# Triangular inverses of a two-layer decoder: 16x16 diagonal blocks made row by row on VectorE, then three doubling steps instead of six

## The chip, the cores and the metric

The kernel runs on one core of one Trainium2 chip. A core has TensorE (PE: matmuls and transposes, with a separate weight load, PEld), VectorE (DVE), ScalarE (ACT), GpSimd (POOL), SyncE (SP, which issues the DMAs here) and 16 DMA engines. Each engine works through its own instructions in order and waits on semaphores for the others. The metric is the device time of one execution in microseconds; the median of several runs counts.

## The reference

The kernel computes two decoder layers on x of 256 tokens by 2048 features in fp32. Layer 0 mixes tokens with mLSTM heads and RWKV-7 heads, layer 1 with retention heads and gated DeltaNet heads; each mixer is followed by a SwiGLU block.

```python
for layer in range(DEPTH):
    h = x * (1.0 + scale) + shift
    y = _mixer_ab(h, ...) if layer % 2 == 0 else _mixer_cd(h, positions, ...)
    x = _layer_norm(ALPHA * x + (1.0 + gate) * y, ln_g[layer, 0], ln_b[layer, 0])
    y = _swiglu(x * (1.0 + scale) + shift, ffn_w_gate[layer], ffn_w_up[layer], ffn_w_down[layer])
    x = _layer_norm(ALPHA * x + (1.0 + gate) * y, ln_g[layer, 1], ln_b[layer, 1])
```

Two of the mixers are delta rules: the state is corrected at each token by what it already holds. RWKV-7 has it as a recurrence, DeltaNet in chunks with a triangular solve:

```python
S = S * wt[:, :, None, :] + sa[..., None] * bt[:, :, None, :] + vt[..., None] * kt[:, :, None, :]   # sa = S at
...
ut = jnp.eye(CHUNK, dtype=f32) + jnp.where(strict, jnp.einsum('cbhtd,cbhsd->cbhts', kb, kc) * gamma, 0.0)
u = lax.linalg.triangular_solve(ut, vc * bc[..., None], left_side=True, lower=True)
```

The kernel writes both in chunks of 128 tokens, and so needs, for each head and chunk, the inverse of a 128x128 unit triangular matrix. There are 16 RWKV heads and 8 DeltaNet heads, two chunks each.

## The kernel before

**Products.** Every large product goes through `product` and `unit` (L342 to L368). A unit takes 512 rows of a weight matrix, 1 MB, by DMA into one of three `raw` buffers. `split` (L327) makes two halves of it: ScalarE rounds a half to fp32r (`hi`, L337) and VectorE makes the rest (`lo = raw - hi`, L338); there are three buffers of each. Per half TensorE runs four groups of three matmuls (L357 to L359: activations' high part by `hi` and by `lo`, low part by `hi`) into two PSUM banks of the kind `g`, of which there are four. Between units, `fill` puts in the modulation's products: 1 MB of `ada` weights goes through the same `raw` buffers, and one VectorE instruction multiplies and sums it (L289).

**Order.** The program is traced in order, and a scheduler sorts the instructions into each engine's queue ahead of the run by priority, which is the place in the program; `high_priority(offset=n)` moves a block n instructions ahead. The splits have an offset of 2000. What comes later in the program, such as a following product, is put beside earlier work where its buffers allow it. On the chip each queue is then run strictly in that order.

**The heads.** `rwkv` (L864) takes the 16 RWKV heads in four batches of four heads. `rwkv_batch` and `rwkv_front` prepare a batch (L708, L724 to L761), with the transposes of the columns in `rwkv_tiles` (L691). `rwkv_heads` (L763) computes the scores (L776), copies them with ScalarE into `mk[:, 0]` and `mk[:, 1]` (L777, L778), masks them with GpSimd (`keep_upper` L642, `unit_diagonal` L646), calls `inverses` on `mk[:, 0]` (8 matrices: four heads by two chunks) and goes on with the state and the output (L794 to L848). `gdn_group` (L1051) does the same for two groups of four DeltaNet heads, with the scores written by VectorE into `ma[:, 0]` (L1109) and the inverse used at L1136; `ma[:, 1]` is used at L1141.

**The inverse.** `inverses` (L600) keeps the inverse `d` and its transpose `dt`, each 128 x 8 x 128, and doubles the size of the inverted diagonal blocks. Start: eight transposes of `mt` (L611), of which VectorE keeps the 2x2 blocks (L612, mask `m2`), while GpSimd keeps those of `mt` itself in `dt` (L613, mask `m2t`). Then follow six levels, for block sizes 2, 4, 8, 16, 32 and 64. A level multiplies `mt` by the blocks (L622), masks (L626, `lev`), multiplies by `dt` (L629), adds into `d` (L632), transposes `d` (L636) and copies it into `dt` with ScalarE (L637). Each level works on two halves of four matrices. A 128x64 fp32 matmul is two instructions in the trace, so a level has 16 of L622, 16 of L629 and 8 of L636.

Of the kernel before, what the change touches and what calls it, by code (L numbers as in the profile page):

```python
# [13 lines left out]
AF = mybir.ActivationFunctionType  # L14
ALU = mybir.AluOpType
# [4 lines left out]
P = 128  # L20
# [9 lines left out]
LN_EPS = 1e-5  # L30
DH = 128
DECAY = -math.exp(-0.5)
LEVELS = (2, 4, 8, 16, 32, 64)


COLS = {}
# [7 lines left out]

CONS = {}
_n = 0
for _name, _w in [("ident", 128), ("cum", 256), ("tr", 128), ("ones", 128), ("sl", 128), ("m2", 128), ("m2t", 128),
                  ("lev", 64 * len(LEVELS)), ("bones", 128), ("hsel", 2), ("freq", 64)]:
    CONS[_name] = (_n, _w)
    _n += _w  # L50
# [3 lines left out]
def constants():  # L54
    i = np.arange(P)
    c = np.zeros((P, NCONS), np.float32)

    def put(name, a):
        o, w = CONS[name]
        c[:, o:o + w] = a  # L60

    u, t = i[:, None], i[None, :]
# [4 lines left out]
    put("tr", u <= t)  # L67
    put("ones", 1.0)
    put("sl", u > t)
    put("m2", (u // 2 == t // 2) & (t <= u))  # L70
    put("m2t", (u // 2 == t // 2) & (u <= t))
    lev = []
    for b in LEVELS:
        j = np.arange(64)
# [6 lines left out]
    s, t = i[:, None].astype(np.float64), np.arange(T)[None].astype(np.float64)  # L81
    ret = np.zeros((8, P, 384), np.float32)
    for h in range(8):
        lg = np.log1p(-np.exp2(-5.0 - h))
        e = np.where(t >= s, np.exp(lg * np.maximum(t - s, 0.0)), 0.0) * DH ** -0.5
# [100 lines left out]
class Trunk:  # L186
# [413 lines left out]
    def inverses(self, mt, dd):  # L600


        nc, v = self.nc, self.nc.vector
        d, dt = dd[:, 0], dd[:, 1]
        halves = [slice(0, 4), slice(4, 8)]
        m2, m2t = (self.con(n).unsqueeze(1).to_broadcast([P, 4, P]) for n in ("m2", "m2t"))
        four = lambda x: x.rearrange("p (h t) -> p h t", h=4)
        for hs in halves:
            b = self.bank()
            for j in range(4):  # L610
                nc.tensor.transpose(b[:, P * j:P * j + P], mt[:, hs.start + j, :], self.ident)  # L611
            v.tensor_tensor(d[:, hs, :], four(b[:]), m2, ALU.mult)  # L612
            nc.gpsimd.tensor_tensor(dt[:, hs, :], mt[:, hs, :], m2t, ALU.mult)  # L613
        lev = self.con("lev")
        for n, size in enumerate(LEVELS):
            dv = d.rearrange("p h (n two b) -> p h n two b", two=2, b=size)
# [23 lines left out]
    def keep_upper(self, x, dims, strict):  # L640

        self.nc.gpsimd.affine_select(x, x, pattern=[[0, n] for n in dims] + [[1, P]], compare_op=ALU.is_gt if strict else ALU.is_ge,  # L642
                                     fill=0.0, base=0, channel_multiplier=-1)

    def unit_diagonal(self, x, n):
        self.nc.gpsimd.affine_select(x, x, pattern=[[0, n], [1, P]], compare_op=ALU.not_equal, fill=1.0, base=0, channel_multiplier=-1)  # L646


    def shifted(self, out, src, mu, rows=P):
# [113 lines left out]
    def rwkv_heads(self, B):  # L763
# [6 lines left out]
        for t in range(NT):  # L770
            for c, h in heads:
                r = slice(64 * h, 64 * h + 64)
                j = 4 * t + 2 * c + h
                b = self.bank()
                for x in range(2):
                    mm(b[:, T * x:T * x + T], bk[r, c, x, t, :], ar[r, c, t].rearrange("p x s -> p (x s)"), start=True, stop=True)  # L776
                nc.scalar.activation(mk[:, 0, j, :], b[:, 0:P], AF.Copy, scale=rho[:, t, 2 * c + h:2 * c + h + 1])  # L777
                nc.scalar.activation(mk[:, 1, j, :], b[:, 2 * P:3 * P], AF.Copy)  # L778
                v.tensor_copy(rbkr[:, j], b[:].rearrange("p (k x s) -> p k x s", k=2, x=2)[:, :, 1, :])
            js = slice(4 * t, 4 * t + 4)  # L780
            self.keep_upper(mk[:, :, js, :], [2, 4], True)
            self.unit_diagonal(mk[:, 0, js, :], 4)
            self.keep_upper(rbkr[:, js], [4, 2], False)
        dt = self.inverses(mk[:, 0], self.y8([P, 2, 8, P]))
        V = B["vb"][:, 0]
# [265 lines left out]
    def gdn_group(self, g, product, rest, gates=None):  # L1051
# [43 lines left out]
        for t in range(NT):  # L1095
# [13 lines left out]
                    v.scalar_tensor_tensor(ma[:, 0, 4 * t + i + j, :], bv[:, j, 0, :], wn[:, t, i + j:i + j + 1], gam[:, i + j, :], ALU.mult, ALU.mult)  # L1109
                v.tensor_tensor(ma[:, 1, 4 * t + i:4 * t + i + 2, :], bv[:, :, 1, :], gam[:, i:i + 2, :], ALU.mult)  # L1110
            js = slice(4 * t, 4 * t + 4)
            self.keep_upper(ma[:, 0, js, :], [4], True)
            self.unit_diagonal(ma[:, 0, js, :], 4)
            self.keep_upper(ma[:, 1, js, :], [4], False)
        dt = self.inverses(ma[:, 0], self.a8([P, 2, 8, P]))
        rest()
# [233 lines left out]
```

## Time and profile before

| | |
|---|---|
| median of the runs | 2915.05 us |
| lowest and highest of 3 runs | 2909.9, 2915.27 us |
| the profiled execution | 2917.53 us |
| its span, first to last instruction | 2914.8 us |
| mean granted clock of TensorE | 0.976 |
| calls of `inverses` | 4 (RWKV), 2 (DeltaNet) |
| the calls, first L611 to last L636 start | 230 to 279, 319 to 364, 407 to 451, 501 to 546, 1691 to 1738, 1823 to 1875 us |

The profile is of one execution on the chip. In a row of groups stand the line, the engine, the operation, output<-input with their shapes, the count, then the busy time in us and the mean of one in ns, and behind a second bar the idle time of the engine just ahead of those instructions with what ended it. In a timeline a row begins with its start and its length in us; a bracket gives the idle time before it and its releaser. Weight loads lie beside matmuls, and a matmul's length holds the time that it takes through the array, so the issue time of a batch is read from the start of what follows. Durations below are of this execution.

### The profile page before, as it was taken

Reading aid. Unit: us, or ns where it says so; the run is one execution under the profiler, and the core shown is the slowest. Engines: PE = TensorE matmul, PEld = TensorE weight load, DVE = VectorE, ACT = ScalarE, POOL = GpSimd, SP = SyncE. Lnnn points to the kernel's source line nnn. Section 1 sums busy time; section 2 is a strip of 40 time slices with the busy share of each in tenths; the row PEclk is TensorE's granted clock in tenths of the full one; section 3 lists DMA queues with packets and bytes.
Section 4 is the critical chain, followed back from the end, with each engine's and each line's share of the span. In section 5 each row is a group of like instructions: output and inputs, shape, how many; then the busy total and the mean of one; then the engine's idle time right before and its main releaser. Section 6 shows DMA issues by size and latency. Waiting matters only on the chain.

```text
span 2914.8 us, 34843 instructions
## 1 busy us (share of the span) xinstructions
PE 2760.8 (95%) x13466; PEld 2291.6 (79%) x13466; DVE 2011.9 (69%) x2955; ACT 1276.3 (44%) x1685; POOL 123.5 (4%) x114
## 2 busy tenths in 40 slices
PE   3699999999999999999998999999989999999997
PEld 2578887877778888888887888877878888888886
DVE  7876666687777557767758878687786545556556
ACT  2264345446454444444445545343444444443442
POOL 0001111020000000000000121101000000000000
PEclk9799999999999999999999999999999999999998
DMA  9974234367578668867855756477656656667563
GB/s 366 356 277 170 91 134 159 131 242 267 199 249 305 249 219 296 297 236 275 305 197 205 295 209 241 159 277 295 216 202 231 249 195 224 242 220 241 192 216 130
DMA packets 106189, 674.62 MB, mean 231 GB/s; under 512 B 12068, under 2 KB 14248, under 8 KB 28328
## 3 DMA queue, kind: packets, MB, share of 16 engines
q1 hardware_dynamic: 106024, 672.41, 64.1%
q8 instruction: 105, 1.72, 0.2%
q14 instruction: 60, 0.49, 0.0%
HBM read 663.97 MB, written 8.39 MB: 231 GB/s over the span
## 4 chain that ended last, share of the span: by engine, by line
PE 62%; DVE 5%; DMA 3%; issue 1%; ACT 1%; POOL 1%; POOLq 0%; DVEq 0%; ACTq 0%
PE g L359 19%; PE g L358 19%; PE g L357 19%; DMA raw<-ada 2%; DVE lo L338 2%; DVE raw L289 1%; PE m L622 1%; PE m L629 1%; PE m L575 1%; ACT hi L337 1%; DMA raw<-gu 1%; DMA raw<-w_cd 0%; PE m L524 0%; PE c L317 0%; PE m L636 0%
## 5 line engine op out<-in xcount | busy, mean ns | idle before, releaser
L338 DVE TENSOR_TENSOR lo<-raw,hi 128x1024 fp32r<-128x1024 f32 (+2 forms) x848 | 1025.4, 1215 | 653.6 <-ACT hi L337 650.3
L337 ACT ACTIVATE hi<-raw 128x1024 fp32r<-128x1024 f32 (+2 forms) x848 | 885.7, 1049 | 1165.6 <-PE g L359 1004.1
L357 PE MATMUL g<-hi,h 128*128 128x512 f32 (+3 forms) x2368 | 932.7, 396 | 80.3 <-ACT hi L337 76.5
L358 PE MATMUL g<-lo,h 128*128 128x512 f32 (+3 forms) x2368 | 934.1, 395 | 3.8 <-DVE lo L338 3.8
L359 PE MATMUL g<-hi,h 128*128 128x512 f32 (+3 forms) x2368 | 930.9, 394 | 0.0
L357 PEld LDWEIGHTS g<-hi,h 128*128 128x128 f32 x2368 | 451.9, 191 | 172.0 <-ACT hi L337 78.8
L358 PEld LDWEIGHTS g<-lo,h 128*128 128x128 f32 x2368 | 452.6, 191 | 95.2 <-DVE lo L338 9.1
L359 PEld LDWEIGHTS g<-hi,h 128*128 128x128 f32 x2368 | 452.0, 191 | 88.6 <-issue 2.7
L289 DVE SCALAR_TENSOR_TENSOR raw<-raw,silu_c 128x2048 f32<-128x2048 f32 x176 | 404.4, 2298 | 23.1 <-DMA raw<-ada 22.8
L359 PE MATMUL g<-hi,a 128*128 128x512 f32 x960 | 374.5, 390 | 0.0
L357 PE MATMUL g<-hi,a 128*128 128x512 f32 x960 | 374.4, 390 | 0.0
L358 PE MATMUL g<-lo,a 128*128 128x512 f32 x960 | 374.1, 390 | 0.1
L358 PEld LDWEIGHTS g<-lo,a 128*128 128x128 f32 x960 | 180.3, 188 | 37.4 <-DVE lo L338 0.5
L359 PEld LDWEIGHTS g<-hi,a 128*128 128x128 f32 x960 | 180.3, 188 | 36.9
L357 PEld LDWEIGHTS g<-hi,a 128*128 128x128 f32 x960 | 180.2, 188 | 37.0
L1099 POOL TENSOR_SCALAR s<-cons_sb,log_alpha 128x128 f32<-128x128 f32 x16 | 22.9, 1446 | 1040.6 <-PE g L359 903.4
L637 ACT ACTIVATE y<-m 128x512 f32<-128x512 f32 x48 | 27.4, 595 | 78.3 <-PE m L636 78.1
L902 DVE SCALAR_TENSOR_TENSOR f<-c,cols_sb,f 128x255 f32<-128x255 f32 (+2 forms) x120 | 57.2, 477 | 6.2 <-ACT f L900 5.1
L626 DVE TENSOR_TENSOR P<-m,cons_sb 128x256 f32<-128x256 f32 x72 | 30.1, 423 | 43.6 <-PE m L622 43.2
L629 PEld LDWEIGHTS m<-P,y 128*128 128x128 f32 x384 | 50.0, 203 | 2.1 <-issue 0.3
L622 PEld LDWEIGHTS m<-y,a 128*128 128x128 f32 x384 | 49.7, 205 | 0.8
L622 PE MATMUL m<-y,a 128*128 128x64 f32 x384 | 49.7, 283 | 0.0
(376 smaller groups left out, 2051.2 us busy)
## 6 DMA issues: line engine op xcount, KB each, us to landing
raw<-ada SPq DMA_DIRECT2D x176, 1024.0 KB, 5.5
raw<-gu SPq DMA_DIRECT2D x176, 1024.0 KB, 4.8
raw<-dn SPq DMA_DIRECT2D x88, 1024.0 KB, 4.8
raw<-w_cd SPq DMA_DIRECT2D x60, 1024.0 KB, 5.0
raw<-w_ab SPq DMA_DIRECT2D x56, 1024.0 KB, 5.5
a<-ada SPq DMA_DIRECT2D x16, 1024.0 KB, 11.3
raw<-o_ab SPq DMA_DIRECT2D x16, 1024.0 KB, 5.0
raw<-o_cd SPq DMA_DIRECT2D x16, 1024.0 KB, 4.9
```

The lines of the kernel that those rows point to most:

```text
L289: v.scalar_tensor_tensor(w[:], w[:], 1.0, self.sc[:], ALU.mult, ALU.mult, accum_out=m[:, i:i + 1])
L337: nc.scalar.activation(hi[:, :2 * n], ws, AF.Copy)
L338: nc.vector.tensor_tensor(lo[:, :2 * n], ws, hi[:, :2 * n], ALU.subtract)
L357: mm(o, ah, wh, start=first, stop=False)
L358: mm(o, ah, wl, start=False, stop=False)
L359: mm(o, al, wh, start=False, stop=stop and k == 3)
L575: nc.tensor.transpose(b[:, P * k:P * k + P], gs[:, t, P * k:P * k + P], self.ident)
L622: nc.tensor.matmul(x[:, 64 * j:64 * j + 64], mt[:, hs.start + j, :], dv[:, hs.start + j, :, 0, :], start=True, stop=True)
L626: v.tensor_tensor(p[-1][:], four(x[:, 0:256]), mask, ALU.mult)
L629: nc.tensor.matmul(x[:, 256 + 64 * j:320 + 64 * j], dt[:, hs.start + j, :], y[:, j, :], start=True, stop=True)
L637: nc.scalar.activation(dt[:, hs, :], four(x[:]), AF.Copy)
L902: v.scalar_tensor_tensor(o[:, d:T], z[:, 0:T - d], self.col(wname, c + 3 - d), o[:, d:T], ALU.mult, ALU.add)
```

## The change

The inverses of the 16x16 diagonal blocks are made on VectorE, and the doubling starts at size 16. Per call:

- `e2` takes the two 16x16 diagonal blocks of each 32x32 diagonal block of `mt`, for 32 partitions at a time, times a strictly triangular mask (`tri`); their sum `u` holds, for each partition, the row of its own block, 128 x 8 x 16.
- `e` starts as `u` plus the unit diagonal (`diag`). For k from 14 down to 1 a shuffle brings row k of each block to all 16 partitions of the block, the copy is multiplied by column k of `u`, and the product is added into `e`, all for the columns beyond k. That block has a priority offset of 4000.
- `dt` is `e` spread over the block diagonal by the mask `blk`, and `d` its transpose by TensorE, copied by ScalarE.
- The levels of sizes 2, 4 and 8 go, and with them their part of `lev`, the masks `m2` and `m2t`, GpSimd's product at L613, and `unit_diagonal`. `keep_upper` stays for the second matrix alone (`mk[:, 1]`, `ma[:, 1]`); the first is now read without a mask.

```diff
-LEVELS = (2, 4, 8, 16, 32, 64)
+BASE = 16
+LEVELS = (16, 32, 64)
...
-    put("m2", (u // 2 == t // 2) & (t <= u))
-    put("m2t", (u // 2 == t // 2) & (u <= t))
+    c32, c16 = np.arange(32)[None], np.arange(BASE)[None]
+    put("tri", (u % 32 // BASE == c32 // BASE) & (u % BASE < c32 % BASE))
+    put("diag", u % BASE == c16)
+    put("blk", u // BASE == np.arange(P // BASE)[None])
...
     def inverses(self, mt, dd):
         nc, v = self.nc, self.nc.vector
         d, dt = dd[:, 0], dd[:, 1]
         halves = [slice(0, 4), slice(4, 8)]
-        m2, m2t = (self.con(n).unsqueeze(1).to_broadcast([P, 4, P]) for n in ("m2", "m2t"))
         four = lambda x: x.rearrange("p (h t) -> p h t", h=4)
+        with self.tc.high_priority(offset=4000):
+            e2 = self.t1([P, 8, 2, BASE])
+            for q in range(4):
+                r = slice(32 * q, 32 * q + 32)
+                o = CONS["tri"][0]
+                v.tensor_tensor(e2[r], mt[r, :, r].rearrange("p h (a c) -> p h a c", a=2),
+                                self.cons[r, o:o + 32].rearrange("p (a c) -> p a c", a=2).unsqueeze(1).to_broadcast([32, 8, 2, BASE]), ALU.mult)
+            u, e, f = (self.own([P, 8, BASE], "e1", 3) for _ in range(3))
+            v.tensor_tensor(u[:], e2[:, :, 0, :], e2[:, :, 1, :], ALU.add)
+            v.tensor_tensor(e[:], u[:], self.con("diag").unsqueeze(1).to_broadcast([P, 8, BASE]), ALU.add)
+            for k in range(BASE - 2, 0, -1):
+                n = BASE - 1 - k
+                x = f[:, :, k + 1:]
+                v.stream_shuffle(x, e[:, :, k + 1:], [k] * 16 + [16 + k] * 16)
+                v.tensor_tensor(x, x, u[:, :, k:k + 1].to_broadcast([P, 8, n]), ALU.mult)
+                v.tensor_tensor(e[:, :, k + 1:], e[:, :, k + 1:], x, ALU.add)
         for hs in halves:
+            v.tensor_tensor(dt[:, hs, :].rearrange("p h (n c) -> p h n c", c=BASE), e[:, hs, :].unsqueeze(2).to_broadcast([P, 4, 8, BASE]),
+                            self.con("blk").unsqueeze(1).unsqueeze(3).to_broadcast([P, 4, 8, BASE]), ALU.mult)
             b = self.bank()
             for j in range(4):
-                nc.tensor.transpose(b[:, P * j:P * j + P], mt[:, hs.start + j, :], self.ident)
-            v.tensor_tensor(d[:, hs, :], four(b[:]), m2, ALU.mult)
-            nc.gpsimd.tensor_tensor(dt[:, hs, :], mt[:, hs, :], m2t, ALU.mult)
+                nc.tensor.transpose(b[:, P * j:P * j + P], dt[:, hs.start + j, :], self.ident)
+            nc.scalar.activation(d[:, hs, :], four(b[:]), AF.Copy)
...
-            self.keep_upper(mk[:, :, js, :], [2, 4], True)
-            self.unit_diagonal(mk[:, 0, js, :], 4)
+            self.keep_upper(mk[:, 1, js, :], [4], True)
...
-            self.keep_upper(ma[:, 0, js, :], [4], True)
-            self.unit_diagonal(ma[:, 0, js, :], 4)
             self.keep_upper(ma[:, 1, js, :], [4], False)
```

More of the change, by code (lines that the diff above doesn't have):

```diff
@@ L46 @@
 _n = 0
-for _name, _w in [("ident", 128), ("cum", 256), ("tr", 128), ("ones", 128), ("sl", 128), ("m2", 128), ("m2t", 128),
+for _name, _w in [("ident", 128), ("cum", 256), ("tr", 128), ("ones", 128), ("sl", 128), ("tri", 32), ("diag", 16), ("blk", 8),
                   ("lev", 64 * len(LEVELS)), ("bones", 128), ("hsel", 2), ("freq", 64)]:
@@ L643, in keep_upper @@
                                      fill=0.0, base=0, channel_multiplier=-1)
-    def unit_diagonal(self, x, n):
-        self.nc.gpsimd.affine_select(x, x, pattern=[[0, n], [1, P]], compare_op=ALU.not_equal, fill=1.0, base=0, channel_multiplier=-1)
     def shifted(self, out, src, mu, rows=P):
```

## The prediction

> **What bounds the kernel now.** I read the page's busy shares first, then its chain, then the two stages that call `inverses`, then the waits of TensorE there.
>
> ```profile
> PE 2760.8 (95%) x13466; PEld 2291.6 (79%) x13466; DVE 2011.9 (69%) x2955; ACT 1276.3 (44%) x1685; POOL 123.5 (4%) x114
> ...
> PE 62%; DVE 5%; DMA 3%; issue 1%; ACT 1%; POOL 1%; POOLq 0%; DVEq 0%; ACTq 0%
> ...
> L338 DVE TENSOR_TENSOR lo<-raw,hi 128x1024 fp32r<-128x1024 f32 (+2 forms) x848 | 1025.4, 1215 | 653.6 <-ACT hi L337 650.3
> L337 ACT ACTIVATE hi<-raw 128x1024 fp32r<-128x1024 f32 (+2 forms) x848 | 885.7, 1049 | 1165.6 <-PE g L359 1004.1
> L289 DVE SCALAR_TENSOR_TENSOR raw<-raw,silu_c 128x2048 f32<-128x2048 f32 x176 | 404.4, 2298 | 23.1 <-DMA raw<-ada 22.8
> ```
>
> TensorE (PE) is busy 95% of the span and carries 62% of the chain that ended last; VectorE (DVE) carries 5%. ScalarE's `hi` copies wait 1004.1 us for TensorE to finish with a buffer (L359): the three split buffers are usually full, so weights wait for TensorE and not the other way round. What is taken from TensorE's queue is therefore worth its full length wherever other work can move up. The stages that matter, by windows of all engines:
>
> ```profile
> 230.00:560.00 330.00, 317.60 (x2052) 274.40 (x2053) 202.28 (x463) 145.79 (x279) 39.47 (x36) 0.96 0.36 127
> 1690.00:1880.00 190.00, 185.72 (x1126) 160.57 (x1124) 140.25 (x254) 80.19 (x129) 27.60 (x24) 0.97 0.54 195
> ```
>
> The columns are PE, weight loads, DVE, ACT, POOL, granted clock, DMA share. Four calls of `inverses` lie in the first window, two in the second. TensorE is busy 96% and 98%, VectorE 61% and 74%, the DMA engines 36% and 54%. So inside the stages too TensorE is the bound, and VectorE has some room, though not much in the second. The idle rest of TensorE has mostly one cause:
>
> ```profile
> L611 PE MATMUL m<-cons_sb,a 128*128 128x128 f32 x48 | 8.1, 297 | 16.9 <-POOL a L646 16.9
> L646 POOL TENSOR_SCALAR_AFFINE_SELECT a<-a 128x512 f32<-128x512 f32 x12 | 17.6, 1465 | 0.4
> ...
> 230.22 0.66 PE L611 MATMUL m<-cons_sb,a 128*128 128x128 f32 x4 [1.93 <-POOL a L646]
> 235.15 0.66 PE L611 MATMUL m<-cons_sb,a 128*128 128x128 f32 x4 [2.59 <-POOL a L646]
> ```
>
> The first transposes of each inverse (L611) wait for GpSimd's masks, 16.9 us in all six calls.
>
> **What the change takes from TensorE.** One level in the first call, in the timeline of TensorE; what stands behind each batch gives its issue time:
>
> ```profile
> 265.42 1.90 PE L622 MATMUL m<-y,a 128*128 128x64 f32 x16
> 267.13 0.47 PE L358 MATMUL g<-lo,h 128*128 128x512 f32 x1
> ...
> 268.14 1.89 PE L629 MATMUL m<-P,y 128*128 128x64 f32 x16
> 269.84 0.47 PE L359 MATMUL g<-hi,h 128*128 128x512 f32 x1
> ...
> 270.39 1.03 PE L636 MATMUL m<-cons_sb,y 128*128 128x128 f32 x8
> 271.26 1.90 PE L622 MATMUL m<-y,a 128*128 128x64 f32 x16
> ```
>
> The steps are 267.13 - 265.42 = 1.71 us, 269.84 - 268.14 = 1.70 us and 271.26 - 270.39 = 0.87 us: 4.28 us per level. Three levels fewer (2, 4 and 8) in six calls are 18 x 4.28 = **77.0 us**. The first eight transposes of a call stay; only their source changes from `mt` to `dt`.
>
> The masks on POOL leave the path: `mt` goes into the new chain, and into L622, unmasked (the level masks `lev` clear the rest), so the **16.9 us** of waits go. POOL's remaining mask of `mk[:, 1]` or `ma[:, 1]` serves L794 or L1141, after the inverse, and is costed at nothing: the levels hide it; without them its price would be that of such a mask, 1.5 us. The constants shrink by 392 columns, 128 x 392 x 4 bytes = 0.2 MB; by
>
> ```profile
> DMA packets 106189, 674.62 MB, mean 231 GB/s; under 512 B 12068, under 2 KB 14248, under 8 KB 28328
> ```
>
> that is 0.9 us at most, at the start; I count nothing.
>
> **What it adds on VectorE.** Prices, from dependent small operations on 128x8 (start to start) and from larger ones by size:
>
> ```profile
> 301.00 0.17 DVE L412 TENSOR_TENSOR v<-v 128x8 f32<-128x8 f32 x1
> 301.20 0.17 DVE L413 TENSOR_TENSOR v<-v,v 128x8 f32<-128x8 f32 x1
> 301.40 0.17 DVE L414 TENSOR_SCALAR v<-v 128x8 f32<-128x8 f32 x1
> ...
> L626 DVE TENSOR_TENSOR P<-m,cons_sb 128x256 f32<-128x256 f32 x72 | 30.1, 423 | 43.6 <-PE m L622 43.2
> ...
> L612 DVE TENSOR_TENSOR y<-m,cons_sb 128x512 f32<-128x512 f32 x8 | 5.5, 690 | 8.9 <-PE m L611 8.9
> L632 DVE TENSOR_TENSOR y<-m,y 128x256 f32<-128x256 f32 x48 | 20.3, 424 | 25.2 <-PE m L629 24.8
> ```
>
> The slope is (690 - 423) / 256 = 1.04 ns per element; a dependent operation on 128x8 takes 0.20 us from start to start, so its fixed part is 0.192 us. The chain has 14 rows, k from 14 to 1, each a shuffle, a product and a sum on 8 x n elements, n from 1 to 14: 42 x 0.192 + 3 x 840 x 0.00104 = 8.1 + 2.6 = 10.7 us. Ahead of it are four 256-element products (4 x 0.42 = 1.7 us, as L626) and two 128-element sums (0.33 us each): 13.1 us. No row shows a shuffle. I bound it by 0.17 us (L413's duration, already in the sum) and by twice that if a lane list is loaded first, 14 x 0.17 = 2.4 us more; I take the middle, so the chain is **14.3 us** (13.1 to 15.5) of VectorE time per call. The two `blk` products (0.69 us) replace the two of L612. Gone are six L626 and six L632, 12 x 0.42 = 5.1 us. Net +9.2 us per call, 55 us in all: VectorE would go from 2012 to about 2067 us. ScalarE loses six L637 copies and gains two of the same shape:
>
> ```profile
> L637 ACT ACTIVATE y<-m 128x512 f32<-128x512 f32 x48 | 27.4, 595 | 78.3 <-PE m L636 78.1
> ...
> 228.94 0.29 ACT L778 ACTIVATE a<-m 128x128 f32<-128x128 f32 x1
> ...
> 256.93 1.00 PE L622 MATMUL m<-y,a 128*128 128x64 f32 x8
> ```
>
> That is 2.4 us less per call, on an engine with room: nothing.
>
> The Trainium skill speaks against the trade: VectorE: DVE Perf Modes, section "Rules for kernel authors", says of chained DVE operations to keep their count low, since each pays its fixed part. The trace agrees, with 0.192 of 0.20 us fixed on 128x8. By that page's 2400 ns for a shuffle of 2048 elements, less 2048 x 1.04 ns, a shuffle's fixed part is an estimated 0.27 us; the sum would stay as it is.
>
> **What of it lies on the path.** In call one the last score copy (L778) ends at 229.2 us, and the size-16 level, which stays, starts at 256.9 us (L622): 27.7 us. After the change the same stretch holds about 1 us until VectorE is free (half of a 2.3 us L289), 14.3 us of chain, 0.7 us of `blk` product: 16 us to the first transpose, then 1 to 2 us of transposes and copies. So the latency shortens as well, but TensorE now needs 16 us of other work where it has no level to do. Queued behind the chain on VectorE (it has priority 4000, the splits 2000) are L338's `lo` halves and L289; whoever waits for `lo` is the product on TensorE. Its cover is the three full split buffers, 12 matmuls each:
>
> ```profile
> 248.65 0.39 PE L358 MATMUL g<-lo,h 128*128 128x512 f32 x1
> 248.88 0.40 PE L359 MATMUL g<-hi,h 128*128 128x512 f32 x1
> ...
> 237.39 0.63 PE L358 MATMUL g<-lo,h 128*128 128x512 f32 x1
> 237.82 0.63 PE L359 MATMUL g<-hi,h 128*128 128x512 f32 x1
> ```
>
> At 0.23 us from start to start that is 36 x 0.23 = 8.3 us, and some 2.7 us of the next batch's L708, L691 and L724, 11 us in all. So I put a wait of 16 - 11 = **5 us per call**, 30 us in six. Both ends: nothing, if splits slip in between the dependent rows of the chain and keep TensorE fed; 16 us, if TensorE finds nothing at all.
>
> **The sum.** -77.0 - 16.9 + 30 = -63.9 us. Its profiled execution took 2917.5 us (span 2914.8), which gives 2853.6; the median of the runs, 2915.05, lies 2.5 us lower, so I forecast **2851 us**.
>
> The slow clock after a wait is costed at nothing, since there are waits before and after. Its price: behind the waits at 230 and 235 us the products start 0.43 us apart instead of 0.23 (last fence), and the granted clock of 0.96 over the 330 us of four calls makes 330 x 0.04 / 4 = 3.3 us per call. The Trainium skill, in TensorE: Matmul & The Clock Gate, section "Part 1: The HAM clock gate", puts the slow half at idle windows of some 3.4 us; here two shorter gaps, 1.93 and 2.59 us with some work between, were followed by it, so the trace asks for less. By the page a 5 us wait would always pay it, by the trace also.
>
> **Rivals.**
> (a) The chain is wholly covered: splits are issued between its dependent rows, as other work stands between the steps of a root here:
>
> ```profile
> 297.67 0.17 DVE L409 TENSOR_SCALAR v<-v 128x8 int32<-128x8 int32 x1
> 297.74 0.42 DVE L748 TENSOR_TENSOR y<-f,f 128x256 f32<-128x256 f32 x1
> 298.08 0.16 DVE L410 TENSOR_SCALAR v<-v 128x8 int32<-128x8 int32 x1
> ...
> DVE  7876666687777557767758878687786545556556
> ```
>
> Then -77.0 - 16.9 = -93.9 us, and without the slow clock up to -93.9 - 6 x 3.3 = -114: 2801 to 2821 by the runs, say 2815. For it: L748 starts 0.07 us behind L409, so each dependent step leaves 0.13 us free. Against: it needs nearly all of VectorE's room.
>
> (b) VectorE becomes the bound of the two stages. Its work there would be 202.3 + 4 x 9.2 = 239 us and 140.3 + 2 x 9.2 = 159 us. The last row above is its busy share in fortieths of the span: 8 tenths at most. At 80% the stages take 299 and 199 us in place of 330 and 190: 31 - 9 = 22 us less, 2893. For it: 74% now in the second stage. Against: L289s can move to later products.
>
> (c) Slower: a transpose placed in TensorE's queue ahead of ready products stands there for the whole chain, and they behind it. Price: 16 us and 3.3 us of slow clock per call, 116 us; -93.9 + 116 = +22 us, 2937. It decides from 93.9 / 6 = 15.7 us of lost time per call. For it: L611 stood so for POOL. Against: POOL's waits average 16.9 / 6 = 2.8 us per call, and the buffers are full.
>
> (d) It doesn't do what it says: the freed 77 us is only waited out elsewhere, since the head work behind each inverse sets the pace; within 0.2%, 2915. Against: TensorE 96% busy.
>
> **How the numbers follow.** Forecast 0.52, (a) 0.22, (b) 0.15, (c) 0.07, (d) 0.04. Measurement of this kernel tells some 0.2% (6 us) from no change. Faster is the forecast, (a) and most of (b), 0.88; same is (d) and a little of (b), 0.05; slower is (c), 0.07. The range goes from 2810, within (a), to 2893, the price of (b); a third of (a), some of (b), and (c) and (d) stay outside, about 0.2.
>
> **What would show it.** Right: no L622, L629 or L636 for three levels (576, 576 and 288 instructions become half); no POOL releaser at the first transposes; VectorE near 2067 us; TensorE's busy time some 77 us less, weight loads and matmuls together; waits of a few us, on VectorE or the `dt` product, ahead of six groups of transposes; levels starting some 18 to 25 us after the last L778. Wrong: rows of the chain far above 0.2 to 0.3 us; long gaps of TensorE beside the chain with L338 late; the granted clock lower in both stages; VectorE past 85% there.

## The result, and the profile after

| | before | after |
|---|---|---|
| median of 4 runs, us | 2915.16 (2909.9 to 2918.53) | 2867.9 (2864.73 to 2871.11) |
| profiled execution, us (span) | 2917.53 (2914.8) | 2870.56 (2868.8) |
| mean granted clock | 0.976 | 0.969 |
| TensorE busy, us | 2760.8 | 2692.8 |
| VectorE busy, us | 2011.9 | 2041.5 |
| first layer norm, behind layer 0's mixer, starts at, us | 794.74 | 776.21 |
| layer 1's mixer, from the start of the second norm to that of the third, us | 603.4 | 574.2 |

The kernel is faster by 1.6%: the ratio is 0.984, with an interval of 0.9819 to 0.986. That is 47 us, where 64 were forecast; the time lies inside the range of 2810 to 2893. The last two rows of the table say where the 17 us are missing. The two calls of `inverses` in layer 1 brought 29 us, about 14.6 each. The four in layer 0 brought 18.5 us, 4.6 each.

The page of after, its busy shares, the granted clock in fortieths of the span, and the chain that ended last:

```profile
PE 2692.8 (94%) x12746; PEld 2215.4 (77%) x12746; DVE 2041.5 (71%) x3255; ACT 1263.7 (44%) x1664; POOL 82.5 (3%) x86
...
PEclk9799798899999999999999999999999999999998
...
PE 77%; DVE 14%; DMA 5%; issue 2%; ACT 2%; POOL 0%; POOLq 0%; SPq 0%; DVEq 0%; ACTq 0%
```

TensorE is still the bound, but VectorE carries 14% of the chain in place of 5%, and the granted clock falls to 7 and 8 tenths in the fifth, seventh and eighth slice (290 to 360 and 430 to 570 us), which lie in layer 0. The same row before has a 9 in all of them:

```profile
PEclk9799999999999999999999999999999999999998
```

The same two stages by windows of all engines (us, then PE, weight loads, DVE, ACT, POOL, granted clock, DMA share, GB/s), before:

```profile
170.00:794.70 624.70, 605.64 (x3374) 502.11 (x3374) 441.24 (x896) 302.33 (x505) 64.59 (x62) 0.98 0.51 184
1600.00:2150.00 550.00, 534.99 (x2806) 449.34 (x2804) 435.85 (x740) 249.99 (x353) 58.75 (x48) 0.98 0.66 240
```

and after, each window ending at the same event:

```profile
170.00:776.20 606.20, 562.96 (x2891) 453.04 (x2890) 464.45 (x1096) 295.34 (x490) 41.23 (x46) 0.94 0.52 189
1581.50:2103.70 522.20, 509.64 (x2566) 423.79 (x2566) 443.18 (x841) 245.27 (x346) 41.08 (x36) 0.98 0.69 253
```

In layer 1 TensorE's busy time fell by 25.4 us, the six levels of two calls (6 x 4.28 = 25.7), and its idle time (window less busy) from 15.0 to 12.6 us: the change worked there as if it were covered completely. In layer 0 the twelve levels should have taken 51.4 us off TensorE. Its busy time fell by only 42.7, so what stayed ran 8.7 us slower (granted clock 0.94 in place of 0.98), and its idle time grew from 19.1 to 43.2 us, though the waits for POOL are gone. -51.4 + 8.7 + 24.1 is the 18.6 us that the stage got shorter.

What TensorE waited for, in the view of waits of after (total us, times, longest):

```profile
PE m L853 <- ACT t L848: 8.6, 2, 8.0
PE g L361 <- DVE lo L341: 7.9, 15, 1.2
PE c L708 <- DVE e L624: 7.7, 2, 5.9
PE c L911 <- DVE v L418: 7.6, 1, 7.6
...
PE c L708 <- DVE e L625: 3.7, 1, 3.7
...
PE m L632 <- DVE y L628: 0.2, 1, 0.2
```

L632 are the first transposes of an inverse, where I expected waits of 5 us per call: they wait 0.2 us in all. The waits are at other places, in the work that follows the inverses of layer 0: at the tail (L853), at the token transposes of a later product (L708) and at the conv (L911). Here is why, in the timeline of VectorE in the middle of call one's rows (start, duration):

```profile
236.31 0.18 DVE L624 STREAM_SHUFFLE e<-e 128x16 f32<-128x16 f32 x1
236.39 2.27 DVE L292 SCALAR_TENSOR_TENSOR raw<-raw,silu_c 128x2048 f32<-128x2048 f32 x1
...
238.59 0.17 DVE L625 TENSOR_TENSOR e<-e,e 128x16 f32<-128x16 f32 x1
238.68 1.21 DVE L341 TENSOR_TENSOR lo<-raw,hi 128x1024 fp32r<-128x1024 f32 x1
239.82 0.17 DVE L626 TENSOR_TENSOR e<-e,e 128x16 f32<-128x16 f32 x1
...
243.53 0.19 DVE L625 TENSOR_TENSOR e<-e,e 128x32 f32<-128x32 f32 x1
243.75 0.19 DVE L626 TENSOR_TENSOR e<-e,e 128x32 f32<-128x32 f32 x1
```

Two dependent operations of a row can start 0.22 us apart (last two lines). But in the order in which VectorE's queue was laid out, a modulation row of 2.27 us or a `lo` half of 1.21 us stands between many of them. The chain of call one starts at 229.12 us and its `blk` product at 267.40 us. The windows of that stretch, for all engines, for L341 and for L292 alone:

```profile
229.00:268.40 39.40, 36.02 (x159) 28.07 (x159) 38.74 (x101) 16.88 (x21) 2.04 (x3) 1.00 0.79 294
...
229.00:268.40 39.40, 13.38 (x11) 1.00 0.79 294
...
229.00:268.40 39.40, 11.64 (x12) 1.00 0.79 294
```

VectorE is busy 38.74 of 39.40 us, 13.38 of them with splits and 11.64 with the modulation. TensorE meanwhile is fed (36.0 of 39.4 us, clock 1.00). From the chain's start to the first transposes call one takes 39.3 us, the other calls of layer 0 20.1, 28.8 and 29.1 us, those of layer 1 54.5 and 41.5 us. So no wait stands at the transposes, and in three of layer 0's four calls the inverse is late instead. From the last score copy to the tail's first matmul (L794 before, L810 after) the four calls took 50, 47, 44 and 46 us before, and 66, 43, 51 and 57 us after; the second, with the shortest chain, comes a little sooner. TensorE has nothing else to do when the tail, the token transposes and the next batch come late:

```profile
316.19 0.47 PE L853 MATMUL m<-cons_sb,t 128*128 128x128 f32 x1 [7.97 <-ACT t L848]
...
336.90 1.09 PE L708 MATMUL c<-cons_sb,zt 128*128 128x128 f32 x4 [3.69 <-DVE e L625]
...
434.53 1.09 PE L708 MATMUL c<-cons_sb,zt 128*128 128x128 f32 x4 [5.88 <-DVE e L624]
...
500.38 1.09 PE L911 MATMUL c<-cons_sb,zt 128*128 128x128 f32 x4 [7.63 <-DVE v L418]
```

The releaser that stands behind L708 is a row of the next inverse, but the transposes don't read it. They need a bank of PSUM (`c`) that the token shift (L670, with L669 on ScalarE) has read, and L670 stands among the rows on VectorE. The timeline of all engines shows it, with the wait of L669 in brackets:

```profile
432.80 0.47 DVE L670 SCALAR_TENSOR_TENSOR z<-c,cols_sb,z 128x255 f32<-128x255 f32 x1
...
433.30 0.47 ACT L669 ACTIVATE z<-c,one_less_mu 128x256 f32<-128x256 f32 x1 [3.56 <-DVE z L670]
...
433.91 0.48 DVE L670 SCALAR_TENSOR_TENSOR z<-c,cols_sb,z 128x255 f32<-128x255 f32 x1
434.31 0.01 DVE L624 LOAD_MASK_SELECT e<-e  x1
```

The last L670 ends at 434.39 us, and L708 starts at 434.53. Around such gaps the clock is low: a window of all engines over the first of them shows TensorE busy for 25.59 us of 40, at 0.66.

```profile
300.00:340.00 40.00, 25.59 (x108) 18.52 (x108) 21.58 (x85) 13.56 (x41) 3.93 (x5) 0.66 0.17 60
```

### The profile page after: what moved, and what is told of

Read it like the earlier page. It is cut to its first block, busy times and chain, and to the rows that moved or that the text cites. A ratio compares the mean times of both kernels' runs of the same rounds, so it can differ in the third digit from the quotient of the medians.

```text
span 2868.8 us, 33529 instructions
## 1 busy us (share of the span) xinstructions
PE 2692.8 (94%) x12746; PEld 2215.4 (77%) x12746; DVE 2041.5 (71%) x3255; ACT 1263.7 (44%) x1664; POOL 82.5 (3%) x86
## 4 chain that ended last, share of the span: by engine, by line
PE 77%; DVE 14%; DMA 5%; issue 2%; ACT 2%; POOL 0%; POOLq 0%; SPq 0%; DVEq 0%; ACTq 0%
PE g L361 22%; PE g L362 22%; PE g L360 22%; DVE lo L341 4%; DVE raw L292 4%; DMA raw<-ada 2%; ACT hi L340 1%; PE m L642 1%; PE m L649 1%; DMA raw<-gu 1%; DVE a L292 1%; PE m L793 1%; PE m L578 1%; PE m L656 1%; DMA a<-ada 1%
## 5 line engine op out<-in xcount | busy, mean ns | idle before, releaser
L341 DVE TENSOR_TENSOR lo<-raw,hi 128x1024 fp32r<-128x1024 f32 (+2 forms) x848 | 1022.5, 1211 | 626.4 <-ACT hi L340 623.9
L292 DVE SCALAR_TENSOR_TENSOR raw<-raw,silu_c 128x2048 f32<-128x2048 f32 x176 | 405.0, 2302 | 29.7 <-DMA raw<-ada 29.0
L1115 POOL TENSOR_SCALAR s<-cons_sb,log_alpha 128x128 f32<-128x128 f32 x16 | 18.6, 1177 | 1040.7 <-PE g L362 884.6
L530 ACT ACTIVATE t<-m,affine 128x128 f32<-128x128 f32 x96 | 35.1, 476 | 29.9 <-PE m L527 29.9
L403 ACT ACTIVATE t<-t,affine 128x256 f32<-128x256 f32 x16 | 8.7, 589 | 75.9 <-DVE affine L301 75.9
L292 DVE SCALAR_TENSOR_TENSOR a<-a,silu_c 128x2048 f32<-128x2048 f32 x16 | 36.6, 2287 | 0.4 <-DMA a<-ada 0.3
L527 PE MATMUL m<-cons_sb,y 128*128 128x128 f32 x96 | 16.7, 317 | 18.4 <-DVE v L495 18.4
L662 POOL TENSOR_SCALAR_AFFINE_SELECT a<-a 128x512 f32<-128x512 f32 (+1 forms) x20 | 20.7, 1040 | 454.2 <-ACT a L795 410.1
```

The costliest lines, as they stand in the source:

```text
L292: v.scalar_tensor_tensor(w[:], w[:], 1.0, self.sc[:], ALU.mult, ALU.mult, accum_out=m[:, i:i + 1])
L341: nc.vector.tensor_tensor(lo[:, :2 * n], ws, hi[:, :2 * n], ALU.subtract)
L530: nc.scalar.activation(h32[:, j, :], b[:, P * j:P * j + P], AF.Identity, bias=self.ab[:, 16 + k:17 + k], scale=self.ab[:, k:k + 1])
```

## The experiments

The theory after this reading is **S**: the 14 dependent rows are spread out between other VectorE work, the inverse ends late, and in layer 0, where one batch follows another, TensorE pays with idle time and slow clock. Its first rival is **L**: it is VectorE's added load itself, work that delays splits and evictions, whoever waits for the rows. Later ones are named where they come up. All runs in one table (ratio against the kernel before, measured on the same chip; "norm" is the start of the first layer norm, behind layer 0's mixer, in the profiled execution, 794.74 before and 776.21 after):

| run | median us | ratio (95%) | norm, us |
|---|---|---|---|
| after | 2867.9 | 0.984 (0.9819 to 0.986) | 776.2 |
| e1, DeltaNet alone | 2886.75 | 0.9907 (0.989 to 0.9923) | 794.8 |
| e2, no rows | 2809.78 | 0.9646 (0.963 to 0.9662) | 724.1 |
| e3, rows aside | 2828.41 | 0.9706 (0.9682 to 0.973) | 741.4 |
| e4, 8x8 blocks | 2859.23 | 0.9818 (0.9801 to 0.9834) | 763.2 |
| e5, rows undisturbed | 2922.01 | 1.0029 (1.0017 to 1.0041) | 797.0 |
| e6, token buffers | 2866.66 | 0.9841 (0.9815 to 0.9868) | 772.2 |
| e7, 8x8 and 16x16 | 2851.89 | 0.9788 (0.9768 to 0.9807) | 760.0 |
| e8, no priority | 2876.11 | 0.987 (0.9854 to 0.9886) | 778.3 |
| e9, modulation later | 2888.63 | 0.9907 (0.9885 to 0.9928) | 787.0 |
| e10, e7 and e9 | 2855.57 | 0.9793 (0.9772 to 0.9813) | 760.8 |
| e11, e9 with transposes | 2865.71 | 0.985 (0.9821 to 0.9878) | 766.9 |
| e12, e7 and e6 | 2862.1 | 0.9843 (0.9802 to 0.9885) | 794.1 |

### e1: the change in the DeltaNet of layer 1 alone

```diff
-        dt = self.inverses(mk[:, 0], self.y8([P, 2, 8, P]))
+        dt = self.inverses_old(mk[:, 0], self.y8([P, 2, 8, P]))
```

The four calls of layer 0 keep the six levels and their masks.

> The RWKV heads keep the old inverse (six levels, GpSimd masks), the DeltaNet groups have the new one; u, e and f share one tile of the t2 kind. Theory S (supply): between the rows of the chain other VectorE work is put, so a call's chain lasts 20 to 40 us instead of its own 13; TensorE spends the ready products in that time, and in layer 0, where only two token buffers and four PSUM banks can hold products ahead, it finds none in the serial tail of the heads. In layer 1 products are never short. S expects layer 1's gain alone, 27.8 us by the two traces (550 to 522.2 us between the layer norms): 2887 us, 2880 to 2895, and layer 0 as before (624.7 us from 170 us to the first norm). Theory L (load): VectorE's additional work itself is the bound, wherever it stands; then the fuller stage, layer 1 (74% busy before), should have gained less than 20 us: above 2895.

It took 2886.75 us: layer 1's two calls bring 28.4 us and layer 0's four the remaining 18.9 (26.2 and 21.1 if e1 is taken from the 2912.93 us of before that were measured beside it). The first norm stands at 794.8 us, as before the change. That is in S's range and below the 2895 us that L asked for. The two stages can be told apart, and nearly all of the loss is in layer 0.

### e2 and e3: the rows left out, and the rows beside the path

e2 leaves out the 14 rows, so the 16x16 blocks aren't inverted:

```diff
-            for k in range(BASE - 2, 0, -1):
...
-                v.tensor_tensor(e[:, :, k + 1:], e[:, :, k + 1:], x, ALU.add)
```

> The 14 rows of the chain are left out (u plus the unit diagonal goes straight into dt, so the 16x16 blocks are not inverted); the three levels and all else are as in the changed kernel. Both S and L expect the rows to be the cost: -77.0 for the levels and -16.9 for the waits of GpSimd are then nearly whole, 2821 to 2835 us, TensorE's granted clock back at about 0.98 in layer 0. If it stays above 2855 us, the lost time lies elsewhere (the d copy on ScalarE, the blk products, the order of the queues).

e3 leaves out the same part of the result, but issues the rows on a copy that nothing reads:

```diff
+            w = e2[:, :, 0, :]
+            v.tensor_copy(w, e[:])
...
-                v.stream_shuffle(x, e[:, :, k + 1:], [k] * 16 + [16 + k] * 16)
+                v.stream_shuffle(x, w[:, :, k + 1:], [k] * 16 + [16 + k] * 16)
...
-                v.tensor_tensor(e[:, :, k + 1:], e[:, :, k + 1:], x, ALU.add)
+                v.tensor_tensor(w[:, :, k + 1:], w[:, :, k + 1:], x, ALU.add)
```

> All 14 rows run, on a copy of e that nothing reads afterwards (one 128-element copy more per call); dt is made of u plus the unit diagonal, as in the run without rows, so the blocks are not inverted and nothing waits for the rows. VectorE's work is that of the changed kernel. S expects nearly the time without rows: within 12 us of it, 2825 to 2843 us. L expects nearly the time of the changed kernel: 2858 to 2872 us.

Without rows the kernel takes 2809.8 us, below what I had expected; the rows cost 58.1 us in all. With the rows there but nobody waiting it takes 2828.4. So 18.6 us are the price of VectorE's load (L), and 39.5 us that of waiting for the rows (S). The time lies in S's range, though S had also said within 12 us of e2: the load costs more than it allowed for. The four runs of e3 lie between 2817.7 and 2833.0 us, and the split is no finer than that. By the first norm, 17.3 and 34.8 us of these are in layer 0. In layer 1 the mixer takes 568.1 us in e2, 571.8 in e3 and 574.2 after: there the rows cost 6.2 us, and waiting for them 2.4. Layer 0's windows, e2 and then e3:

```profile
170.00:724.10 554.10, 543.38 (x2898) 440.99 (x2897) 432.91 (x875) 295.43 (x492) 47.19 (x46) 0.99 0.57 207
```

```profile
170.00:741.40 571.40, 554.66 (x2897) 450.13 (x2896) 456.76 (x1101) 295.66 (x491) 48.66 (x46) 0.97 0.55 201
```

VectorE works the same time in e3 as in after within 2% (456.8 and 464.5 us). TensorE's idle time goes from 10.7 us (e2) to 16.7 (e3) and to 43.2 (after), its busy time on the same matmuls from 543.4 to 554.7 and to 563.0. Most of the idle time belongs to the waiting. One thing e3 doesn't keep: with nobody waiting, the scheduler spreads the rows further, 34 to 43 us from first to last shuffle in layer 0's calls in place of 13 to 31. So the 39.5 us hold the wait together with the order that goes with it. e2 is 105 us faster than before (103 by the before measured beside it), so the levels and the waits for POOL, together with the clock that comes back, are worth no less than the 93.9 us of the prediction.

### e4: blocks of 8x8, six rows and four levels

```diff
-BASE = 16
-LEVELS = (16, 32, 64)
+BASE = 8
+LEVELS = (8, 16, 32, 64)
```

> 8x8 blocks instead of 16x16, and four levels (8, 16, 32, 64): six rows (18 small operations) instead of 14 (42), one more addition of 128 elements ahead, one level of 4.28 us more on TensorE in each call (25.7 us). S: the chain lasts about half as long, so the products last longer beside it; of the 48 us lost in layer 0 (idle +24, slow clock +24) a half to nearly all comes back: 2868 + 26 - 24 to 45 = 2849 to 2870 us. L: VectorE's work falls by some 7 us per call, 42 us in all, of which a half shows: 2868 + 26 - 21 = 2873 us, 2868 to 2880.

2859.23 us, within S's range and below L's. Six more levels on TensorE (25.7 us by the 4.28 us of a level) and eight rows fewer in each chain are together not slower, by the medians 8.7 us faster; the two intervals overlap a little. The first transposes of call one start at 252.0 us in place of 268.4.

### e5: the rows with nothing between them

The chain is issued as one block to which the scheduler adds nothing, with a semaphore of its own:

```diff
+            ins.then_inc(self.vs, 1)
+            v.wait_ge(self.vs, self.vc)
...
+        with self.tc.high_priority(offset=4000), self.tc.tile_critical():
```

> The chain as one critical block with a semaphore of its own: no other VectorE work between its rows, the same operations (48 per call), which should then last 13 to 16 us per call instead of 20 to 45. If the stretch of the chain is what costs layer 0 its 35 us (changed kernel against the rows set aside), the first layer norm comes at 740 to 760 us instead of 776 and the time is 2835 to 2855 us. Rival B (blocked splits): the lo halves wait behind the block, TensorE stands beside it with L341 late, the time is 2868 us or more, waits of TensorE for lo some 10 us or more above the 7.9 us of the changed kernel.

I expected a gain, and it is 54 us slower than after and 0.3% slower than before. The chain itself does what it should: in call one (in a timeline of VectorE) it lasts from 235.16 to 248.56 us, 13.4 us (the prediction had 14.3). But now TensorE stands at the transposes. From the view of waits:

```profile
PE m L639 <- DVE y L635: 52.9, 3, 19.1
PE m L639 <- DVE a L635: 28.3, 2, 14.2
...
PE g L362 <- DVE lo L342: 2.7, 6, 0.7
```

and in the timeline:

```profile
249.85 1.12 PE L639 MATMUL m<-cons_sb,y 128*128 128x128 f32 x4 [18.86 <-DVE y L635]
```

81.2 us in five waits, 13.5 us per call over six: this is rival (c) of the prediction, the transposes ahead of ready products in TensorE's queue. It isn't the wait for `lo` that I had named as the danger of such a block. It doesn't show that an undisturbed chain is bad in itself: the transposes may stand where they do because the scheduler doesn't count the block's length, and that wasn't tried apart.

### e6: is it the supply of products?

A theory on the way: the products that could fill TensorE's gaps in layer 0 are held back by buffers for their results. Two of those take another, larger buffer here.

```diff
+                if blk == 3:
+                    two = self.a8([P, 2, NT, 512])
...
+                tokens.append(self.by_tokens(banks, two[:, blk - 3] if blk < 5 else None))
```

> The changed kernel with the fourth and fifth token blocks of layer 0 in one 8 KB buffer of the a kind instead of the two zt buffers, so that two more products can be made ahead. If the supply of products ahead is what is short in layer 0 (waits at L708 of 11.4 us behind the rows, TensorE idle at 308 to 316 us), a half or more of the 35 us comes back: first norm at 745 to 760 us, 2837 to 2853 us. If the serial tail of the heads sets the pace whatever stands beside, it stays at 2862 to 2873 us; slower than that, the borrowed buffer holds back the next batch's mk.

2866.66 us, no change: in this form the theory isn't borne out. It isn't cleanly refuted either, since the edit opens a gap in TensorE's work at call one. From 200 to 250 us TensorE is busy 31.9 of 50 us at a clock of 0.76, against 48.2 us at 1.00 in after, and the longest wait there is 6.6 us at L708.

### e7: 8x8 in layer 0, 16x16 in layer 1

```diff
-        dt = self.inverses(mk[:, 0], self.y8([P, 2, 8, P]))
+        dt = self.inverses(mk[:, 0], self.y8([P, 2, 8, P]), 8)
...
-        dt = self.inverses(ma[:, 0], self.a8([P, 2, 8, P]))
+        dt = self.inverses(ma[:, 0], self.a8([P, 2, 8, P]), 16)
```

> 8x8 blocks and four levels for the RWKV heads, 16x16 and three for the DeltaNet groups (f lies in the freed part of e2). From the two traces: the first norm at 763 us as with 8x8 (776 with 16x16) and layer 1 at 574 us between its norms as with 16x16 (581 with 8x8), so 2868 - 13 = 2855 us, 2849 to 2861, some 5 us below 8x8 for all.

2851.89 us, 3 us from what S gave, and faster than both kernels: 63 us below before, 16 below after. Each stage has the size that did better there in e4 and after: 8x8 brings the first norm at 763.2 us, 16x16 at 776.2; layer 1's mixer takes 580.6 us with 8x8 and 574.2 with 16x16. Layer 0 by windows:

```profile
170.00:760.00 590.00, 566.79 (x3054) 463.09 (x3053) 451.92 (x989) 300.82 (x499) 45.00 (x46) 0.97 0.54 194
```

TensorE has 163 instructions more there than in after, is idle for 23.2 us in place of 43.2, and gets a clock of 0.97 in place of 0.94.

### e8: the chain without its priority

```diff
-        with self.tc.high_priority(offset=4000):
+        with self.tc.high_priority(offset=0):
```

> The chain's block without its priority offset (0 instead of 4000). S expects its rows to be put off further behind splits and modulation products: a longer chain and the first norm later, 2868 to 2885 us. If the offset is what holds the splits back, the time falls to 2850 to 2862 us.

2876.11 us, 8 us slower. The priority is worth something, but little: it doesn't keep other work from between the rows. From the first to the last shuffle call one takes 33.9 us in place of 30.9, and the other three calls of layer 0 as long as in after, within 1 us.

### e9 and e10: the modulation taken away from the first rows

The modulation L292 in call one's chain (11.64 us) is work for later layers that is spread over the stage. Here the four RWKV calls get none of it, and the group behind them gets more. The theory (P): what lies between the rows is the cause, so taking it away gives the time back.

```diff
-        self.rwkv(h, rate, early)
+        self.rwkv(h, 0.0, early)
...
-            self.mlstm_group(g, self.ins["w_ab"], h, rate)
+            self.mlstm_group(g, self.ins["w_ab"], h, 1.5)
```

> The changed kernel (16x16) with no modulation product put in beside the RWKV heads' products; all 48 of them come beside the mLSTM products (1.5 per unit instead of 1.09). Beside the rows of the first call VectorE spent 13.4 us on splits and 11.5 us on modulation products out of 39.4 us. Theory P (path): layer 0's batches run one after another, the path from the scores to the state through the rows sets the pace of that stage, and what stands between the rows lengthens it. P expects the first call's rows to end some 11 us sooner, those of the third and fourth 5 to 7 us, and the first norm 10 to 25 us earlier than 776 us, unless the mLSTM stage pays for the work moved there (13 x 2.2 = 29 us of VectorE time): 2843 to 2862 us. If the pace is TensorE's or VectorE's total alone, the time stays at 2863 to 2873 us.

2888.63 us: a miss, 21 us slower than after. Call one did as P says: its first transposes start at 238.4 us in place of 268.4, and its tail at 259.2 in place of 294.1. But the modulation came back in the later calls (L292 in 300 to 400 us: 31.0 us in place of 12.4), so the edit moved it rather than took it away: the rows of calls two and three last 32.7 and 29.6 us from first to last shuffle, in place of 13.2 and 18.1. So e9 is no clean test of P. Around 450 us something else cost more. The timeline of TensorE in e9 (its profiled execution is the fastest of its four, 2881.2 us):

```profile
447.14 0.66 PE L632 MATMUL m<-cons_sb,y 128*128 128x128 f32 x4 [0.83 <-DVE y L628]
450.02 0.65 PE L632 MATMUL m<-cons_sb,y 128*128 128x128 f32 x4 [2.22 <-DVE y L628]
```

and its windows, the last one of all engines (TensorE's busy time is the first number behind the length of the window, and the clock stands ahead of the last two):

```profile
460.00:470.00 10.00, 9.79 (x41) 0.50 0.37 116
470.00:480.00 10.00, 10.00 (x45) 0.50 0.53 201
480.00:490.00 10.00, 10.00 (x48) 0.50 0.01 2
490.00:500.00 10.00, 10.00 (x47) 0.50 0.32 107
...
450.00:520.00 70.00, 63.12 (x264) 55.63 (x266) 32.91 (x94) 20.05 (x44) 0.11 (x1) 0.51 0.22 76
```

After two gaps of 0.83 and 2.22 us at an inverse's first transposes, TensorE runs at half clock for 70 us, though from 460 to 500 us it is busy nearly without a pause.

e10 makes the same move in e7's kernel:

> The mixed kernel (8x8 for RWKV, 16x16 for DeltaNet, 2851.9 us) with the modulation products of layer 0 beside mLSTM alone. P expects a smaller gain than with 16x16, since the rows there last 10 to 20 us only: 5 to 15 us, 2837 to 2847 us. No change (2848 to 2856 us) if the stage's pace has passed to something else.

2855.57 us, not to be told from e7's 2851.89. There the move does neither good nor harm, and the gain that P gave doesn't come.

### e11: something for TensorE to do at that place

Theory C: in e9 the clock is what costs, and it falls because TensorE has too little to do at the transposes. e11 is e9 with 16 transposes per call that nothing reads, between the two halves of the first transposes:

```diff
+            if hs.start == 0:
+                b = self.bank()
+                for j in range(16):
+                    nc.tensor.transpose(b[:, P * (j % 4):P * (j % 4) + P], dt[:, j % 4, :], self.ident)
```

> The run with the modulation moved, plus 16 transposes per call whose result nothing reads, put between the two halves of the first transposes (1.76 us of TensorE by 0.11 us each; 10.6 us in all). In that run two gaps of 0.83 and 2.22 us around the third call's first transposes were followed by 70 us at half clock with TensorE 94 to 100% busy. Theory C (clock): such a gap starts the half clock and the small matmuls behind it don't end it; filling most of the gap keeps full clock there, 450 to 520 us at 1.00, and the time falls by up to 35 - 11 us: 2862 to 2878 us. If the low load of the stage itself brings the half clock, it stays, and the time rises by up to 11 us: 2885 to 2902 us.

2865.71 us: 22.9 us faster than e9 by the medians (the ratios, 0.985 and 0.9907, have intervals that don't overlap), with 96 transposes more to do (10.6 us at 0.11 us each, as eight of the prediction's L636 in 0.87). It is no faster than after. The window that held the slow clock, of TensorE in e11:

```profile
450.00:520.00 70.00, 60.92 (x337) 0.79 0.24 86
```

0.79 in place of 0.51, and from 170 us to the first norm 0.96 in place of 0.92. The time came out within C's range, the clock didn't come back wholly (I had said 1.00), and the added instructions also move others in the queues. So C is supported, and the clock and the order aren't fully separated.

### e12: e7 with the token buffers of e6

> The mixed kernel with the fourth and fifth token blocks in one buffer of the a kind. The same edit moved the first norm of the 16x16 kernel by 4 us and its time not at all; expected here 0 to 5 us less than 2851.9 us, or no change (2846 to 2856 us).

A miss: 2862.1 us, 10 us slower than e7. Its profiled execution took 2884.59 us at a mean clock of 0.964, the other three 2859.2 to 2862.29 us at 0.973 to 0.975, so one program can differ by over 20 us with its clock. In the profiled one TensorE stands 6.63 and 4.03 us at call one, at the token transposes (L714) and at a matmul of the next batch (L747), behind VectorE's work among the rows, and the half clock follows. A window of all engines:

```profile
260.00:280.00 20.00, 20.00 (x94) 19.76 (x95) 6.54 (x18) 2.39 (x4) 0.00 (x0) 0.50 0.00 1
```

TensorE is busy without a pause there and gets half the clock, which lasts from 233 to 332 us in that execution. The gap at call one is that of e6, with the same edit. Whether the other three executions have it too, and lose their 7 to 10 us by it, isn't shown.

## Why the prediction held, and which term was off

- **The levels, -77.0 us.** Right. In layer 1 TensorE's busy time fell by 25.4 us for six levels (25.7 by the prediction), and over the program by 68.0 us with the slow clock against it.
- **The waits for POOL, -16.9 us.** Right: the first transposes wait 0.2 us.
- **The chain's own length, 14.3 us per call.** Right in size: 13.4 us where nothing comes between (e5). A shuffle takes 0.17 to 0.30 us; its lane list, which I had allowed up to 0.17 us, is loaded in 14 ns. VectorE's total rose by 29.6 us to 2041.5, in place of 55 to 2067.
- **The wait of 5 us per call, 30 us in all: the step that was mis-sized, and put at the wrong place.** I took the chain to be done in 16 us, by its priority, with 11 us of full split buffers as cover, so that a wait of 5 us would stand at the first transposes. In fact the rows are spread over 20 to 54 us, the transposes hardly wait, and what the inverse, and the readers of PSUM beside it on VectorE, lose in time is paid later. The actual price is 93.9 - 47.3 = 46.6 us in place of 30. It isn't spread evenly: by e1, layer 1's two calls lost little (31.3 us expected without any wait, 28.4 measured), as rival (a) had it, and layer 0's four lost 43.7 (62.6 and 18.9). So 5 us per call were too many in one stage and less than half of the price in the other; that 30 and 46.6 us lie no further apart, and that the time fell inside the range, which reached up to the price of rival (b), is in part luck. I drew the order of VectorE's queue as a priority would set it, while the trace of before already held, in rival (a)'s fence, the pattern that came: long operations between dependent short ones. I read that pattern as cover for TensorE, which it is in layer 1, and not as delay for the inverse, which it is in layer 0, where the next batch and its products hang on the last.
- **"The latency shortens": wrong.** I expected the size-16 level 18 to 25 us after the last score copy. In call one it starts at 269.7 us, 41 us after it, and before it was at 256.9, 28 us after it. In the four calls of layer 0 it was 28, 31, 25 and 29 us before and 41, 22, 30 and 34 us after: sooner in the second call alone.
- **The slow clock, at nothing (3.3 us per call as its price).** Too low in layer 0: the work that stayed took TensorE 8.7 us longer there, 2.2 us per call, and against e2, on the same matmuls, 19.6 us longer (563.0 and 543.4).
- **Rival (b)**, VectorE as the bound, isn't what the loss follows. VectorE is 98 to 99% busy beside the chains of call one and of layer 1's two calls, where TensorE is busy 91 to 97%, and 87 to 96% beside the others. From 1673 to 1875 us in layer 1 it is past the 85% that I had named as a sign of being wrong (179.8 of 202 us), and little was lost there. e3 prices VectorE's load at 18.6 us. **Rival (c)** didn't come with the change, but e5 shows that it is real: 13.5 us per call, and a kernel 0.3% slower than before. **Rival (d)**, that the freed time is waited out elsewhere, is the better half of what happened in layer 0.

What stays open is how much of layer 0's loss is the longer path alone, how much the order of VectorE's queue beside it and how much the clock that drops behind the gaps: e3 changes all three at once, and e11 moves both order and clock.

## What to carry to other kernels

A chain of short dependent operations that is moved to an engine with room can cost more by what stands between its steps than by what they last: count the long operations that the queue will put there, and look at who waits for the chain's end. The same edit can be free in one stage, where other work stands ready, and lose most of its gain in another, where each batch needs the last; so price it by stage, and let each stage have its own size (e7: 8x8 in one, 16x16 in the other, 16 us better than 16x16 in both, 7 better than 8x8 in both). Keeping the chain together by force (e5) only moved the wait here, with its reader standing in front of ready work.

## What the hardware showed that I had not expected

- Half clock can hold while TensorE is busy. In e9 it stayed at 0.50 from 460 to 500 us with 9.8 to 10.0 of each 10 us busy, and in e12's profiled execution over 20 us of full work and 99 us in all. The Trainium skill, in TensorE: Matmul & The Clock Gate, section "Part 1: The HAM clock gate", gives the full clock back after about 3.4 us of busy time; in these two stretches it didn't come. The busy time there was made of short fp32 matmuls with their weight loads, 4 to 5 per us, with none of the products' 128x512 matmuls from 460 to 500 us in e9 and from 260 to 280 us in e12. A count over the fourteen traces, from 170 to 2800 us in the 3.41 us steps of their clock records, points the same way. Of the steps at half clock with TensorE busy for 95% or more, 81 of the 87 with four or more 128x512 matmuls were the last before full clock, and 31 of the 127 with none. At full clock, half clock followed 7 of 8993 such busy steps with four or more, and 11 of 149 with none, so it also sets in where TensorE hardly pauses. No run was made to tell whether the short matmuls are the reason.
- More work made a kernel faster: 96 transposes that nothing reads took 22.9 us off e9, with the queues' order changed as well.
- A shuffle of 8 to 112 fp32 elements per partition costs what any small operation does, by the source view of after (durations in ns, minimum, median, maximum):

```profile
L624 DVE LOAD_MASK_SELECT e<-e x84: 5/14/15, 233.5 to 1847.2; - x84
L624 DVE STREAM_SHUFFLE e<-e x84: 174/221/297, 233.5 to 1847.2; 128x8 f32<-128x8 f32 x6, 128x16 f32<-128x16 f32 x6, 128x24 f32<-128x24 f32 x6, 128x32 f32<-128x32 f32 x6
```

The product and sum at L625 and L626 have medians of 219 and 220 ns.
- A product on 32 partitions gains nothing from the 96 idle ones: the 24 of L616, with 256 elements on 32 partitions, took a median of 418 ns, and the 256 elements on 128 partitions of L626 before the change 423 ns on average.
